# Output projections of a two-layer decoder trunk with the weights stationary and the residual stream as features by tokens

## The chip, the core and the metric

The kernel runs on one core of a Trainium2 chip. The core has five engines with queues of their own: TensorE (PE, with its weight loads shown apart as PEld) multiplies 128x128 stationary blocks with moving blocks of up to 512 columns into PSUM; VectorE (DVE), ScalarE (ACT) and GpSimd (POOL) work on tiles of 128 partitions; SyncE (SP) issues most DMA transfers. SBUF holds the tiles, PSUM has eight banks of 128 x 512 float32, DRAM holds inputs, outputs and a few intermediate tensors. The metric is the device time of one execution in microseconds, as the median of several runs.

## What is computed

A trunk of two layers over x (512 tokens x 2048 features, float32). Layer 0 mixes tokens by retention with 8 heads, layer 1 by latent attention (MLA) with 16 heads. Each layer is a normalised and modulated sub-layer with a gated residual add:

```python
c_act = jax.nn.silu(c)
for i in range(DEPTH):
    mod = (c_act @ ada_w[i] + ada_b[i])[:, None, :]
    shift, scale, gate = jnp.split(mod, 3, axis=-1)
    h = rmsnorm(x, norm_g[i]) * (1.0 + scale) + shift
    j = i // N_MIXERS
    if i % N_MIXERS == 0:
        y = retention_branch(h, positions, ret_w_in[j], ret_gn_g[j], ret_w_out[j])
    else:
        y = mla_branch(h, positions, mla_w_in[j], mla_q_norm_g[j], mla_w_uq[j],
                       mla_kv_norm_g[j], mla_w_ukv[j], mla_w_out[j])
    x = x + gate * y
return rmsnorm(x, final_norm_g)
```

Each branch ends in an output projection: `(silu(g) * y) @ w_out`, 4096 x 2048 in layer 0 and 2048 x 2048 in layer 1.

## The kernel before

**Precision.** Every operand is held as a high and a low part (hi, lo) in a reduced float32 form; `split` makes them with a ScalarE copy (hi, L132) and a VectorE subtraction (lo, L133). A product is three PE passes: hi x hi, hi x lo, lo x hi.

**The sequence.** Layer 0's input projections come first, with 7 products where 8 would be needed for value and gate. Then a list of `Step` objects is worked off (loop at L1499). A step has units of weights (a load on SP's queue and a `prepare`, which splits), a `multiply` for PE, a `follow` for what comes after it, and work placed `beside` it. In step i the loop loads up to three units ahead, prepares the units of step i + 1, does the `form` work on VectorE and ScalarE, multiplies, and then follows. `behind` and `queued` place instructions behind the last one on the named engines; what is written without them the framework may order by its own estimate of readiness.

**Modulation.** `ada_w` is 2048 rows by 6144 columns per layer. `later_modulation` (L840) takes it in pieces of 1024 columns: 16 loads of 512 KB (one row per partition) on SP's queue, and for each one VectorE operation that adds it, scaled by c_act, to `am` (L857). `Step.rows` says how many such loads a step asks for; their additions come in the next step. Buffers for the rows are `bw`, two of them. `sum_modulation` (L863) then sums `am` over the partitions on PE: for shift and scale by eight matmuls of one column (L870), for the gate by two broad products with a block of ones (L877), whose first row goes with the bias through DRAM (`gate_d`) and comes back spread over all partitions. The last two pieces (layer 1's gate) are loaded during the last two gate blocks of layer 2's input (`g23`, L1460, 16 steps), with one row in the first four steps and two in each of the other twelve; what is left is loaded behind the loop (L1546), and the sum stands there too (L1549), ahead of the attention of the first pair of heads in the text (`uq_chunk`, `ukv_chunk`).

**First output projection (o1).** Four rounds n over pairs of heads, each with four column groups r of 512 features (`round_steps`, L1143). The activations `o1_in` (features by tokens) are the stationary operand, in blocks of 128 tokens; the weights move, 512 features wide (`o1_product`, L1133). So a bank holds 128 tokens x 512 features. In the last round groups 3 and 2 end in `x1_out` (L1110): multiply by the gate, add the residual x, square with a sum per token, write x1 to DRAM. Groups 0 and 1 are done together with weights 1024 wide (`wide`): four steps for the first four units, then four steps with one block of tokens each (`one_token`), so that token blocks finish one after the other.

**Between the layers.** `x1_scale` normalises each block of tokens in place, `h2_pair` (L1238) transposes it on PE (four 128x128 transposes per feature block and half of the tokens) and forms the hi and lo parts of h2, modulated, for 256 tokens at a time. The gate projection of layer 2 (`ga`) starts on half of the tokens: `ga_half` multiplies a unit of weights with 256 columns. `front` (L1380) interleaves these halves with the transposes and with `kr_half` (rotary key).

**Second output projection (o2).** `out_projection` (L1553) does the same as o1 with one round: column groups 0 and 1 alone, 2 and 3 together with the last four units (`tail=4`) done bank by bank. `evac` multiplies by the gate and adds x1; `x2_out` squares, sums per token and multiplies by the final gain; `x2_token` (L1811) takes a block of 128 tokens when all its groups are there, computes the factor (POOL's power at L128), scales 2048 features on ScalarE and VectorE and writes them out.

PSUM banks come in two sets of four, `acc` and `aux`.

## Time and profile before

| | us |
|---|---|
| median of 3 runs | 2253.04 (2251.67 to 2254.42) |
| the profiled execution, as a run | 2254.86 |
| its span, first to last instruction | 2253.1 |
| mean granted TensorE clock | 0.989 of full |

The profile is of one execution. A page gives busy times by engine, the span in 40 slices, and the chain of work that ended last; other views list who waited for whom, busy time in chosen windows, groups of equal instructions with their mean time, and single instructions in order of time. In such rows a line number (L1139) is that of the kernel before; `o<-o_whi,o_h` is output and inputs by their names without numbers; a square bracket at the end gives the idle time ahead of an instruction and what ended it. PE's instructions overlap: a matmul is shown with 0.39 us though the next starts 0.23 us after it.

### The profile page before, as it was taken

Reading aid. Unit: us, or ns where it says so; the run is one execution under the profiler, and the core shown is the slowest. Engines: PE = TensorE matmul, PEld = TensorE weight load, DVE = VectorE, ACT = ScalarE, POOL = GpSimd, SP = SyncE. Lnnn points to the kernel's source line nnn. Section 1 sums busy time; section 2 is a strip of 40 time slices with the busy share of each in tenths; the row PEclk is TensorE's granted clock in tenths of the full one; section 3 lists DMA queues with packets and bytes.
Section 4 is the critical chain, followed back from the end, with each engine's and each line's share of the span. In section 5 each row is a group of like instructions: output and inputs, shape, how many; then the busy total and the mean of one; then the engine's idle time right before and its main releaser. Section 6 shows DMA issues by size and latency. Waiting matters only on the chain.

```text
span 2253.1 us, 28084 instructions
## 1 busy us (share of the span) xinstructions
PE 2178.4 (97%) x10238; PEld 1812.8 (80%) x10238; DVE 1601.9 (71%) x2389; ACT 1012.1 (45%) x1526; POOL 113.9 (5%) x201
## 2 busy tenths in 40 slices
PE   5999999999999999999999999989999799999997
PEld 4887888888888888888888888868888588888886
DVE  7988867766676789666777776656867667777545
ACT  5664433434343454434344444454454155555433
POOL 1000000100000000000000000010001000000000
PEclk9999999999999999999999999989999899999999
DMA  9974685767767778664555555633556822235433
GB/s 342 347 241 159 191 296 188 265 217 242 242 218 255 241 247 288 196 203 153 201 185 189 177 182 174 209 100 99 170 194 218 278 80 80 85 98 173 150 126 117
DMA packets 237340, 440.29 MB, mean 195 GB/s; under 512 B 21561, under 2 KB 95377, under 8 KB 237201
## 3 DMA queue, kind: packets, MB, share of 16 engines
q1 hardware_dynamic: 224192, 399.31, 54.6%
q0 software_dynamic: 12576, 38.91, 4.3%
q8 instruction: 80, 1.31, 0.2%
q14 instruction: 60, 0.48, 0.1%
q10 hardware_dynamic: 432, 0.27, 0.0%
HBM read 395.41 MB, written 43.01 MB: 195 GB/s over the span
## 4 chain that ended last, share of the span: by engine, by line
PE 72%; DVE 12%; DMA 7%; ACT 5%; issue 4%; POOL 0%; SPq 0%; ACTq 0%; DVEq 0%; POOLq 0%
PE o L1139 12%; PE qk L160 4%; PE qk L158 4%; PE qk L159 4%; DMA aw<-in_ada_w_dram 2%; DMA mod_aw<-in_ada_w_dram 2%; PE o L158 2%; PE o L160 2%; PE o L159 2%; PE x L696 2%; PE y L696 2%; PE x L697 2%; PE y L697 2%; PE y L695 2%; PE x L695 2%
## 5 line engine op out<-in xcount | busy, mean ns | idle before, releaser
L1139 PE MATMUL o<-o_whi,o_h 128*128 128x512 f32 x488 | 191.0, 391 | 0.0
L1139 PE MATMUL o<-o_whi,o_l 128*128 128x512 f32 x488 | 189.9, 389 | 0.0
L1139 PE MATMUL o<-o_wlo,o_h 128*128 128x512 f32 x488 | 189.9, 389 | 0.0
L857 DVE SCALAR_TENSOR_TENSOR mod_am<-mod_aw,cact,mod_am 128x1024 f32<-128x1024 f32 x120 | 153.6, 1280 | 34.9 <-DMA mod_aw<-in_ada_w_dram 34.8
L158 PE MATMUL qk<-hT,qk_h 128*128 128x512 f32 x448 | 175.3, 391 | 0.0
L160 PE MATMUL qk<-hT,qk_l 128*128 128x512 f32 x448 | 174.6, 390 | 0.0
L159 PE MATMUL qk<-hT,qk_h 128*128 128x512 f32 x448 | 174.3, 389 | 0.0
L133 DVE TENSOR_TENSOR o_wlo<-o_r,o_whi 128x1024 fp32r<-128x1024 f32 x61 | 74.6, 1223 | 75.3 <-ACT o_whi L132 75.3
L133 DVE TENSOR_TENSOR qk_l<-qk_r,qk_h 128x1024 fp32r<-128x1024 f32 x56 | 68.0, 1222 | 64.0 <-ACT qk_h L132 63.7
L1139 PEld LDWEIGHTS o<-o_whi,o_l 128*128 128x128 f32 x488 | 91.6, 188 | 19.2
L1139 PEld LDWEIGHTS o<-o_wlo,o_h 128*128 128x128 f32 x488 | 91.7, 188 | 18.5
L1139 PEld LDWEIGHTS o<-o_whi,o_h 128*128 128x128 f32 x488 | 91.7, 188 | 18.5
L158 PE MATMUL o<-o_w_hi,o_h 128*128 128x512 f32 x256 | 100.1, 391 | 0.0
L159 PE MATMUL o<-o_w_lo,o_h 128*128 128x512 f32 x256 | 99.8, 390 | 0.0
L160 PE MATMUL o<-o_w_hi,o_l 128*128 128x512 f32 x256 | 99.5, 390 | 0.0
L160 PEld LDWEIGHTS qk<-hT,qk_l 128*128 128x128 f32 x448 | 84.1, 188 | 18.5 <-DVE qk_l L133 1.1
L159 PEld LDWEIGHTS qk<-hT,qk_h 128*128 128x128 f32 x448 | 84.1, 188 | 17.8 <-issue 0.5
L158 PEld LDWEIGHTS qk<-hT,qk_h 128*128 128x128 f32 x448 | 84.1, 188 | 17.7 <-ACT qk_h L132 0.2
L132 ACT CAST qk_h<-qk_r 128x1024 fp32r<-128x1024 f32 x56 | 57.9, 1049 | 88.5 <-PE qk L159 73.4
L370 DVE SCALAR_TENSOR_TENSOR am<-aw,cact,am 128x512 f32<-128x512 f32 x118 | 88.7, 752 | 3.6
L160 PE MATMUL g<-h,g_l 128*128 128x512 f32 x232 | 90.6, 391 | 0.6 <-DVE g_l L133 0.6
L158 PE MATMUL g<-h,g_h 128*128 128x512 f32 x232 | 91.0, 392 | 0.0
(1266 smaller groups left out, 5890.8 us busy)
## 6 DMA issues: line engine op xcount, KB each, us to landing
mod_aw<-in_ada_w_dram SPq DMA_DIRECT2D x128, 512.0 KB, 5.3
aw<-in_ada_w_dram SPq DMA_DIRECT2D x128, 256.0 KB, 6.0
o_r<-in_ret_w_out_dram SPq DMA_DIRECT2D x64, 512.0 KB, 4.4
qk_r<-in_ret_w_in_dram SPq DMA_DIRECT2D x112, 256.0 KB, 3.9
g_r<-in_mla_w_in_dram SPq DMA_DIRECT2D x32, 512.0 KB, 4.4
o_w_raw<-in_mla_w_out_dram SPq DMA_DIRECT2D x32, 512.0 KB, 3.7
qk_d<-qk_st POOLq DMA_DIRECT2D x32, 256.0 KB, 4.0
qk_r<-qk_d SPq DMA_DIRECT2D x32, 256.0 KB, 6.1
```

The costliest lines, as they stand in the source:

```text
L132: ACT.copy(hi, src)
L133: DVE.tensor_sub(lo, src, hi.bitcast(F32))
L158: PE.matmul(o, lhs[0], rhs[0], start=first and not seeded, stop=False, skip_group_check=seeded)
L159: PE.matmul(o, lhs[0], rhs[1], start=False, stop=False, skip_group_check=seeded)
L160: return PE.matmul(o, lhs[1], rhs[0], start=False, stop=last, skip_group_check=seeded)
L370: DVE.scalar_tensor_tensor(out=am, in0=aw[:, k % 2], scalar=ck, in1=am, op0=ALU.mult, op1=ALU.add)
L695: PE.matmul(banks[b], a[0], w[0], start=first, stop=False, skip_group_check=True)
L696: PE.matmul(banks[b], a[0], w[1], start=False, stop=False, skip_group_check=True)
L697: PE.matmul(banks[b], a[1], w[0], start=False, stop=True, skip_group_check=True)
L857: DVE.scalar_tensor_tensor(out=am, in0=aw, scalar=ck, in1=am, op0=ALU.mult, op1=ALU.add)
L1139: PE.matmul(o, a[i], w[j][:, ki, cols], start=first and i + j == 0, stop=last and i == 1, skip_group_check=True)
```

## The change

The residual stream is kept as features by tokens in both output projections, so that 128 features stand on the partitions of a bank and 512 tokens along it:

- Weights are the stationary operand, activations the moving one. x is also handed over transposed (`x_t`), and the output comes in blocks (half of the tokens, 256 features) that the host only rearranges.
- The gate of a layer is a column of 128 features per block (`gate_c`), summed like shift and scale; its way through DRAM and the loads that spread it go. Gate and residual add are one fused VectorE operation (`scalar_tensor_tensor`).
- The sum of squares per token is a sum over partitions: squares are added up in one tile (`ss1`, `ss2`), `token_sums` sums it with matmuls of one column, `token_factors` forms the inverse roots and puts them on diagonals, `spread` multiplies ones with a diagonal, which leaves the factor of each token on all partitions of a bank.
- h2 needs no transposes: `h2_pair` takes two feature blocks for half of the tokens, by fused operations with the factor from PSUM.
- The last columns (four units of weights) are done by halves of the tokens, 256 columns each: `tail0` to `tail3` in o1, `o2_end` in o2, with the norm of the first half among the products of the second.
- `front` has three steps; kr is loaded, multiplied (all tokens at once) and used later.
- The rows of the last two pieces of `ada_w` are asked for two to a step from the first of the 16 steps, with buffers `bw` and `pt` in turn (`pt` has four); the last sum stands behind `uq_chunk` and `ukv_chunk` of the first pair.
- `form_input` and `latent_parts` form the low part by one fused operation.

```diff
-    def later_modulation(pool, pieces, tags=("bm", "bw")):
+    def later_modulation(pool, pieces, tags=("bm", (("bw", 2),))):
...
+            ps = aux(f"{name}_ps")
+            for b in range(8):
+                PE.matmul(ps[:, b : b + 1], am[:, b // 4, b % 4 * P : (b % 4 + 1) * P], crow, start=True, stop=True)
...
+    def token_sums(ps, ss, n0, n):
+        for t in range(n0, n0 + n):
+            PE.matmul(ps[:, t : t + 1], ss[:, t * P : (t + 1) * P], crow, start=True, stop=True)
+
+    def token_factors(ps, n0, n, name):
+        r = rsqrt(ps[:, n0 : n0 + n], n, 1.0 / D, name)
+        diag = tmp(f"{name}_diag")
+        for t in range(n):
+            DVE.tensor_scalar(
+                out=diag[:, t * P : (t + 1) * P], in0=ident, scalar1=r[:, t : t + 1], scalar2=None, op0=ALU.mult
+            )
+        return diag
+
+    def spread(ps, diag, n0, n):
+        for t in range(n):
+            PE.matmul(ps[:, (n0 + t) * P : (n0 + t + 1) * P], ones, diag[:, t * P : (t + 1) * P], start=True, stop=True)
...
-    def x1_out(r, t):
-        g, v = tmp(f"o1_g{r}_{t}"), x1_block(t, r)
-        DVE.tensor_mul(g, o1_banks[3, r, t], o1_gates[r])
-        DVE.tensor_add(v, g, o1_res[t, r])
-        junk = tmp(f"x1_sq{t}_{r}")
-        ACT.activation(junk, v, AF.Square, accum_out=ss1[t][:, r : r + 1])
-        POOL.dma_start(x1_d[t * P : (t + 1) * P, r * T : (r + 1) * T], v)
+    def x1_out(r, b, half=None):
...
+        DVE.scalar_tensor_tensor(
+            out=v, in0=o1_banks[3, r, b][:, cols], scalar=gate_c[0][:, kt : kt + 1], in1=o1_res[b, r][:, cols],
+            op0=ALU.mult, op1=ALU.add,
+        )
+        if half != 0:
+            POOL.dma_start(x1_d[kt * P : (kt + 1) * P, :], whole_)
...
+        sq = tmp(f"x1_sq{r}_{b}_{half}")[:, cols]
+        ACT.activation(sq, v, AF.Square)
+        return lambda: DVE.tensor_add(ss1[0][:, cols], ss1[0][:, cols], sq)
...
-                o, a[i], w[j][:, ki, cols], start=first and i + j == 0, stop=last and i == 1, skip_group_check=True
+                o, w[i][:, ki, c0 + b * P : c0 + (b + 1) * P], a[j], start=first and i + j == 0, stop=last and i == 1,
...
+    block[3].follow = lambda: outs(3, range(4))
+    def second_out():
+        outs(2, range(4))
+        for b in range(4):
+            seed(3, 1, b)
+    block[7].follow = second_out
...
+    def norm_sums(half):
+        if half == 0:
+            norm2["s"] = aux("x1_sums")
+        token_sums(norm2["s"], ss1[0], 2 * half, 2)
...
+    def h2_pair(u, half):
...
+            DVE.scalar_tensor_tensor(
+                out=t, in0=x1[u][:, kt % 2, cols], scalar=a_col[1][:, kt : kt + 1], in1=norm2["r"][:, cols],
+                op0=ALU.mult, op1=ALU.mult,
+            )
...
+            ACT.activation(hi, t, AF.Identity, bias=b_col[1][:, kt : kt + 1])
...
+                DVE.scalar_tensor_tensor(
+                    out=lo, in0=t, scalar=b_col[1][:, kt : kt + 1], in1=hi.bitcast(F32), op0=ALU.add, op1=ALU.subtract
+                )
...
+    def tail2():
+        tail_block(1, 0, 1)
+        queued(out_behind, 1, 0, 1)
+        norm_sums(0)
+        queued(norm_factors, 0)
+        tail_block(1, 1, 1)
+        queued(out_behind, 1, 1, 1)
+        tail_block(1, 2, 1)
+        norm_spread(0)
+        queued(out_behind, 1, 2, 1)
+        lows = queued(h2_pair, 0, 0)
+        tail_block(1, 3, 1)
+        queued(out_behind, 1, 3, 1)
+        queued(lows)
...
+    def front0():
+        ga_half(0, 0)
+        norm_sums(1)
+        queued(norm_factors, 1)
+        queued(h2_pairs, (2, 0))
+        ga_half(1, 0)
+        norm_spread(1)
+        queued(h2_pairs, (0, 1), (1, 1), (2, 1))
+
+    front = [Step() for _ in range(3)]
...
+    front[1].multiply = lambda: (ga_half(2, 0), ga_half(0, 1), queued(h2_pairs, (3, 0), (3, 1), (4, 0)))
+    front[2].multiply = lambda: (ga_half(1, 1), ga_half(2, 1), queued(h2_pairs, (4, 1), (5, 0), (5, 1)))
+    steps += front + ga[3:]
+    ga[3].beside["form"].append(lambda: h2_pairs((6, 0), (6, 1)))
+    ga[4].beside["form"].append(lambda: h2_pairs((7, 0), (7, 1)))
+    ga[6].units.append((kr_load, kr_prepare))
+    ga[6].beside["multiply"].append(kr_products)
...
-    g23 = g2_steps(2, rows=lambda u: 1 if u < 4 else 2) + g2_steps(3, rows=lambda u: 2)
+    g23 = g2_steps(2, rows=lambda u: 2) + g2_steps(3, rows=lambda u: 2)
...
-        yield from later_modulation(pools["l2"], [(1, 2, n) for n in range(2)])
+        yield from later_modulation(pools["l2"], [(1, 2, n) for n in range(2)], ("bm", (("bw", 2), ("pt", 4))))
...
-    sum_modulation(0)
-    use_modulation()
...
     run(uq_chunk(0, *tiles_[:2]))
     run(ukv_chunk(0, *tiles_[2:]))
-    pending = None
+    sum_modulation(0)
+    use_modulation()
...
+    def o2_out(kt, ps, half=None):
...
+        DVE.scalar_tensor_tensor(
+            out=v, in0=ps[:, cols], scalar=gate_c[1][:, kt : kt + 1], in1=o2_res[kt][:, cols],
+            op0=ALU.mult, op1=ALU.add,
+        )
...
+            sq = tmp(f"x2_sq{kt}_{half}")[:, cols]
+            ACT.activation(sq, v, AF.Square)
+            DVE.tensor_add(ss2[:, cols], ss2[:, cols], sq)
+        ACT.activation(v, v, AF.Identity, scale=final_c[:, kt : kt + 1])
...
+    def o2_final(half):
+        cols = slice(half * H, (half + 1) * H)
+        for j in range(KD // 2):
+            v = x2[j][:, :, cols]
+            DVE.tensor_mul(v, v, factor2[:, cols].unsqueeze(1).to_broadcast([P, 2, H]))
+            nc.sync.dma_start(out[half, j], v)
+
+    for b in range(8):
+        o2_end(b, 0)
+    o2_end(0, 1)
+    sums2_ = acc("x2_sums")
+    token_sums(sums2_, ss2, 0, 2)
+    diag = token_factors(sums2_, 0, 2, "x2_0")
+    o2_end(1, 1)
+    factor2 = acc("x2_r")
+    o2_end(2, 1)
+    spread(factor2, diag, 0, 2)
+    o2_final(0)
+    for b in range(3, 8):
+        o2_end(b, 1)
+    token_sums(sums2_, ss2, 2, 2)
+    spread(factor2, token_factors(sums2_, 2, 2, "x2_1"), 2, 2)
+    o2_final(1)
```

`tail0` and `tail1` do the first half of the tokens for groups 1 and 0, `tail3` the second half for group 0 with `h2_pair(1, 0)` between its blocks; each `tail_block` is four units by three passes, 256 columns wide. `o2_end` is the same for a bank of o2 and calls `o2_out`.

457 lines of the change are left out of this document (210 added, 247 removed).

## The prediction

> **What bounds the kernel now.** I read the page first: the busy shares, the granted clock and the chain.
>
> ```profile
> PE 2178.4 (97%) x10238; PEld 1812.8 (80%) x10238; DVE 1601.9 (71%) x2389; ACT 1012.1 (45%) x1526; POOL 113.9 (5%) x201
> PEclk9999999999999999999999999989999899999999
> PE 72%; DVE 12%; DMA 7%; ACT 5%; issue 4%; POOL 0%; SPq 0%; ACTq 0%; DVEq 0%; POOLq 0%
> ```
>
> TensorE (PE) is busy for 97% of the span, so time can only come from fewer matmul columns or from the few places where PE stands still. 2253.1 - 2178.4 = 74.7 us are idle in all. Two of the forty slices have a lower clock; the second view, PE's waits, says why.
>
> ```profile
> PE xT_ps L476 <- ACT x L453: 17.5, 4, 10.5
> PE mod_ps L877 <- DVE mod_am L857: 10.7, 1, 10.7
> PE x1T L1246 <- DVE h2f L1263: 8.9, 3, 5.7
> PE pT L1689 <- ACT p L1676: 5.5, 7, 0.9
> ```
>
> The first belongs to the start and the fourth to attention, which the diff leaves alone. The second (the sum of the modulation) and the third (the transposes of the residual stream between the layers) stand at lines that it rewrites. The third view gives both places, a dense stretch for comparison, and the end.
>
> ```profile
> 1480.00:1510.00 30.00, 19.85 (x91) 15.52 (x90) 18.97 (x37) 15.36 (x30) 5.65 (x10) 0.80 0.33 114
> 1730.00:1750.00 20.00, 20.00 (x88) 16.26 (x88) 12.98 (x12) 5.96 (x9) 2.70 (x5) 1.00 0.90 315
> 1790.00:1810.00 20.00, 10.83 (x31) 7.35 (x32) 10.84 (x11) 3.70 (x7) 1.00 (x2) 0.62 0.52 168
> 2240.00:2253.10 13.10, 0.00 (x0) 0.00 (x0) 5.72 (x13) 3.63 (x6) 1.54 (x2) 0.59 0.40 160
> ```
>
> Columns: length, busy time of PE, weight load, DVE, ACT and POOL, clock, DMA share, GB/s. PE is idle for 10.2 us in the first window, 9.2 us in the third and all 13.1 us at the end; after an idle stretch its clock is low too (0.80, 0.62).
>
> **The swap of operands itself is free.** Weights become the stationary operand and activations the moving one; both remain 128x128 against 128x512, three passes each. Units and splits stay as they are, so rounds 0 to 2 of the first output projection and most of the second cost what they cost. Edits with no price, since PE's products cover them: form_input and latent_parts lose one operation of about 0.7 us per block, o2_out has two VectorE operations where three stood (a block's last products take 1.36 us), the gate's trip through DRAM and its eight broadcast loads go, kr's load and products move three steps later and are needed only there. Without that cover o2_out would cost 0.7 us for each block less, never more. These rows give the prices, from one start to the next:
>
> ```profile
> 2237.46 0.39 PE L160 MATMUL o<-o_w_hi,o_l 128*128 128x512 f32 x1
> 2238.14 0.39 PE L160 MATMUL o<-o_w_hi,o_l 128*128 128x512 f32 x1
> 1513.34 0.40 PE L1334 MATMUL g<-h,g_h 128*128 128x256 f32 x2
> 1513.70 0.40 PE L1334 MATMUL g<-h,g_h 128*128 128x256 f32 x2
> ```
>
> Three passes of 512 columns take 0.68 us (0.227 each), three of 256 columns 0.36 us (0.12 each). "Last columns by halves" turns 96 passes into 192 in each projection: 192 x 0.12 - 96 x 0.227 = **+1.3 us, twice**.
> The Trainium skill, "TensorE: Matmul & The Clock Gate", section "Back-to-back issue gap", would make it less: N / 2.4 + 2.5 ns, 109 ns for 256 columns and 216 ns for 512, hence +0.3 us twice and a sum 2 us lower. The rows stand closer to this kernel's fp32 halves, so I keep them.
>
> **Between the layers.** Here PE ends layer 1 and starts the gate projection of layer 2:
>
> ```profile
> 1494.33 0.39 PE L1139 MATMUL o<-o_whi,o_l 128*128 128x512 f32 x1
> 1494.56 0.60 PE L1246 MATMUL x1T<-ident,x 128*128 128x128 f32 x4
> 1510.53 0.78 PE L1334 MATMUL g<-h,g_h 128*128 128x256 f32 x2
> 1540.68 1.03 PE L1246 MATMUL x1T<-ident,x 128*128 128x128 f32 x8
> 1541.47 0.48 PE L158 MATMUL g<-h,g_h 128*128 128x512 f32 x1
> ```
>
> From 1494.56 to 1510.53 PE only transposes or waits: 16.0 us. The other 40 transposes go in five groups of eight, each 0.79 us or a little more (1540.68 to 1541.47): 4.3 us; the cold restart costs about 0.5 us. Removed: **20.8 us**.
>
> What comes instead: the square sums are added over partitions by tiny matmuls, the factor is spread by two 128-column matmuls for each half, and VectorE scales. By the halves' price the 16 added passes are 2 us, with 1.3 us for the 256-column blocks. kr's 64 passes of 256 become 32 of 512: -0.4 us. The new waits I found by walking the queues with these rows:
>
> ```profile
> L1264 DVE TENSOR_TENSOR h<-h2f,h 128x256 fp32r<-128x256 f32 x32 | 12.8, 423 | 13.9 <-ACT h2f L1261 13.4
> L1263 DVE TENSOR_SCALAR h2f<-x1T,a_col,b_col 128x256 f32<-128x256 f32 x16 | 8.7, 543 | 0.3
> L1259 ACT ACTIVATE h<-x1T,b_col,a_col 128x256 fp32r<-128x256 f32 x32 | 17.3, 580 | 12.3 <-PE x1T L1246 12.3
> L133 DVE TENSOR_TENSOR g_l<-g_r,g_h 128x1024 fp32r<-128x1024 f32 x32 | 38.9, 1222 | 15.8 <-ACT g_h L132 15.7
> L1025 DVE SCALAR_TENSOR_TENSOR y<-yT,vcol,sg x4: 745/746/753, 1035.7 to 1039.5; 128x512 f32<-128x512 f32 x4
> 2240.82 0.99 POOL L128 TENSOR_TENSOR x_r<-x_v,mhalf 128x1 f32<-128x1 f32 x1 [5.47 <-DVE x_v L126]
> ```
>
> A half block is 12 passes, 1.44 us on PE. On DVE its x1_out costs a fused operation and an add, 2 x 0.42 = 0.84 us, and each h2 pair four fused operations. No row has the fused operation at 256 columns; it lies between 0.42 (the plain one at 256) and 0.75 us (the fused one at 512, PSUM operand included). I take 0.46, since it reads as many columns as the first row. In tail2 norm_sums(0) takes an aux bank that x1_out(1, 0, 1) must first read; on DVE that stands behind the last x1_out of half 0 and a weight split of 1.22 us, so PE waits about 1.7 us, and behind it all of tail2 does. norm_sums(1) waits 0.3 us after ga_half(0, 0), ga_half(2, 0) 0.6 us for pair (2, 0). Then DVE is ahead: from the start of tail2, pairs 0 to 5 come to 48 x 0.46 + 6.7 (eight x1_out) + 3.2 (two factors, POOL's power in each) + 7.3 (six splits) = 39.3 us, and PE needs pair 5 after eight half blocks, six half units, two whole units and the small products, 11.5 + 17.3 + 10.9 + 2 = 42 us. Waits: 3 us (0 to 13). Added 1.3 + 2 - 0.4 + 3 = 5.9 us: **net -14.9 us**.
> The Trainium skill, "PSUM — Partial Sum Buffer", section "PSUM bank collisions raise a hardware error", says that two engines must not touch one bank in the same partitions at once. norm_spread(1) writes the bank from which DVE reads half 0 for pair (2, 0); kept apart by that rule, PE would wait for the pair's first two operations, and the sum would be 1 us higher. No run so far shows such a pair.
>
> ACT stays below DVE (eight squares and 24 copies of at most 0.58 us, by its row above); the removed in-place scaling waited for x1's DMA, and nothing takes that place. seed(3, 1) now stands behind four squares on ACT instead of one each, and so do the next weights' casts: +0.3 us. The transposed x costs the same 16 loads; three more small loads on POOL and 48 more columns of one copy lie before the start's first weights: nothing.
>
> **The gate of layer 2.**
>
> ```profile
> 1785.17 0.39 PE L159 MATMUL uq<-qT,uq_hi 128*128 128x512 f32 x1
> 1797.74 1.28 DVE L857 SCALAR_TENSOR_TENSOR mod_am<-mod_aw,cact,mod_am 128x1024 f32<-128x1024 f32 x1 [1.68 <-DMA mod_aw<-in_ada_w_dram]
> 1799.17 3.75 PE L877 MATMUL mod_ps<-mod_am,ones 128*128 128x512 f32 x4 [10.70 <-DVE mod_am L857]
> 1801.94 1.42 PE L158 MATMUL uq<-qT,uq_hi 128*128 128x512 f32 x1
> 1807.44 0.40 PE L158 MATMUL uk<-kvT,ukv_hi 128*128 128x512 f32 x1
> mod_aw<-in_ada_w_dram SPq DMA_DIRECT2D x128, 512.0 KB, 5.3
> 925.19 1.84 PE L870 MATMUL mod_ps<-ones,mod_am 128*128 128x1 f32 x16
> 926.89 0.49 PE L695 MATMUL x<-vg_13o_h,hT 128*128 128x512 f32 x1
> ```
>
> From 1785.40 (one pass after the first row) to 1807.44 PE does 16 passes of uq, worth 3.6 us, in 22.0 us: 18.4 us lost. The reason is in the rows' plan: 4 + 8 + 16 = 28 of 32 rows of ada_w are asked for in the 16 steps, the last four follow afterwards, each waiting for its DMA, and the sum (and uq behind it) for the last. The change asks for two from the first step, 32 of 32, with bw and pt buffers in turn, and places the sum behind uq and ukv of pair 0, some 19 us of PE work. The sum as columns takes 1.70 us and a slow start behind it, 1.95 us. DMA: two rows and one unit are 3 x 512 KB in 24 passes, 5.44 us: 289 GB/s, with the gate's writes some 313; the window 1730 to 1750 carries 315 with PE fully busy, so four more such steps should hold. I leave 1 us for a late split: **net -15.5 us** (-7 to -16). The other three gate pieces cost 0.2 us more each as columns than as two broad products: +0.6 us.
>
> **The end.**
>
> ```profile
> 2239.50 0.39 PE L160 MATMUL o<-o_w_hi,o_l 128*128 128x512 f32 x1
> 2247.39 1.15 ACT L1815 ACTIVATE x<-x,x_r 128x1024 f32<-128x1024 f32 x1 [1.64 <-POOL x_r L128]
> L1809 DVE TENSOR_TENSOR x<-x,fg 128x512 f32<-128x512 f32 x16 | 11.0, 689 | 6.7 <-ACT x_sq L1808 6.7
> ```
>
> Today 13.2 us follow the last product. Afterwards: half 0 is scaled by eight multiplies of 0.69 us, 5.5 us on DVE, while PE does five half blocks, 7.2 us. Behind them DVE has five o2_out, 4.4 us if the next fused operation fills the wait for ACT, 6.6 us if not; then sums, POOL's power (0.99), diagonal, spread, 3.3 us; eight multiplies again, 5.5 us; last write 3.4 to 4.5 us (from 2248.54 to the end it is 4.6 us today for twice the bytes). That is 15.7 to 18.8 us behind the last product: +4. PE gets 1.3 us of halves and 1.4 us of sums, spread and a bank wait. **Net +6.7 us** (+4 to +12).
>
> **Sum**, against the profiled execution: -14.9 + 0.3 - 15.5 + 0.6 + 6.7 = -22.8 us of 2253.1 us. That execution took 2254.86 us as a run, 1.8 us above the median of 2253.04; I subtract from the median: **2230 us**.
>
> **Rivals.**
> *The gate's wait only shrinks (2239 us).* The window 1750 to 1770, whose DMA has slack on paper, ran at 265 GB/s:
>
> ```profile
> 1750.00:1770.00 20.00, 20.00 (x85) 15.71 (x85) 12.62 (x12) 4.12 (x4) 1.45 (x3) 1.00 0.77 265
> ```
>
> At that rate a step's loads need 5.9 us against 5.44, 8 us over 16 steps, and PE gets its weights that much later. Against it: PE was full in that very window. The sum not being moved, since instructions seem not to run in the order of the text (uq went ahead of the sum), would cost no more, because the four late rows are gone. 0.12.
> *VectorE takes over between the layers (2242 us).* If the fused operation costs 0.75 us at 256 columns too, pairs 0 to 5 take 53 us, 11 us behind PE, and the last two add 2 x (8 x 0.75 + 1.22 - 5.44) = 3.5 us; 2.5 us of that are waits already counted. For it: L1263 is 28% dearer than L1264 at equal columns. Against: the plain operation falls from 0.69 us (L1809, at 512) to 0.42 (L1264). 0.12.
> *The same place, slower than before (2266 us).* VectorE becomes the bound outright, at 1.1 us per fused operation when one operand stands in PSUM and PE writes beside it: pairs 0 to 5 need 70 us against 42, the last two 9 us more, 36 us of new waiting. From about 0.95 us on it makes the kernel slower by over 0.2%. No row shows such a price (0.75 at 512 with PSUM). 0.08.
>
> **The numbers.** Forecast 0.68, with 2222 to 2238 us as its own range; rivals 0.12, 0.12, 0.08. 0.2% is 4.5 us, about what a measurement of this kernel tells from no change. The upper end, 2245, takes in the first two rivals; with all new waits gone and the end at its cheaper bound it is 2223, and 2220 leaves 3 us below that for VectorE's lighter queue, which I can't price. Faster by over 0.2%: the forecast and nearly all of the first two rivals, 0.86. Slower: 0.08. The rest, where the end and a rival add up, 0.06.
>
> **What would show it.** Right: no PE wait over 2 us between the last o1 product and ga[3]; mod_ps behind ukv of pair 0 without a wait; windows around both at a clock of 1.00; 15 to 19 us behind the last product. Wrong: PE waiting for h2 in ga[3] to ga[7] (VectorE), for g_l or uq_lo before attention (DMA), or a fused operation at 256 columns over 0.6 us.

## The result, and the profile after

The changed kernel takes **2223.68 us** in the median of 4 runs (2223.08 to 2225.20), the kernel before 2252.73 beside it; the ratio is 0.9871 (95% interval 0.9854 to 0.9888), 29.05 us less. The forecast was 2230, with a range from 2220 to 2245. The profiled executions span 2221.8 and 2253.1 us, 31.3 us apart: the one of before lies 2.1 us above the median of its runs, the one of after at its median. The forecast's sum, -22.8 us, was made against the profiled execution of before; measured the same way, between the two profiles, 8.5 us more were saved than that.

The page of the changed kernel (busy times; the clock in 40 slices; the chain of waits by engine):

```profile
PE 2170.8 (98%) x10414; PEld 1819.9 (82%) x10414; DVE 1586.6 (71%) x2397; ACT 998.5 (45%) x1496; POOL 104.2 (5%) x184
PEclk9999999999999999999999999999999999999998
PE 75%; DVE 11%; ACT 5%; issue 5%; DMA 2%; POOL 0%; SPq 0%; DVEq 0%; POOLq 0%; ACTq 0%
```

PE is busy for 7.6 us less, although it has 176 instructions more on record; most of the saving, 23.7 of the 31.3 us, is idle time (74.7 us before, 51.0 after). The two slices with a low clock are gone; the 8 in the last slice is the end, where PE has nothing left to do. Of PE's waits (total, times, longest) the two at mod_ps (10.7) and x1T (8.9) that stood second and third are gone too, and these are what the change brings:

```profile
PE xT_ps L482 <- ACT x L459: 17.2, 4, 10.9
...
PE x_sums L891 <- DVE x_ss L1841: 2.6, 1, 2.6
PE x_r L906 <- DVE x_diag L898: 1.4, 1, 1.4
PE x_r L906 <- DVE h2f L1276: 1.2, 1, 1.2
...
PE x_sums L891 <- DVE x L1127: 0.2, 1, 0.2
```

The first is the old one of the start. To see where the time went, I cut both executions at the same products of PE's timeline. After:

```profile
1058.62 0.39 PE L1161 MATMUL o<-o_h,o_whi 128*128 128x512 f32 x1
...
1493.75 0.28 PE L1161 MATMUL o<-o_h,o_wlo 128*128 128x256 f32 x1
1493.87 0.40 PE L1426 MATMUL g<-h,g_h 128*128 128x256 f32 x2
1593.11 0.50 PE L701 MATMUL xc<-vgc_00e_h,h 128*128 128x512 f32 x1
1761.46 0.39 PE L158 MATMUL uq<-qT,uq_hi 128*128 128x512 f32 x1
2007.42 0.39 PE L160 MATMUL uk<-kvT,ukv_lo 128*128 128x512 f32 x1
2205.78 0.28 PE L1861 MATMUL o<-o_h,o_w_lo 128*128 128x256 f32 x1
```

And before (the last product there is at 2239.50, shown above):

```profile
1059.91 0.39 PE L1139 MATMUL o<-o_whi,o_h 128*128 128x512 f32 x1
1611.65 0.50 PE L695 MATMUL xc<-vgc_00e_h,h 128*128 128x512 f32 x1
1780.86 0.39 PE L158 MATMUL uq<-qT,uq_hi 128*128 128x512 f32 x1
2043.49 0.39 PE L160 MATMUL uk<-kvT,ukv_lo 128*128 128x512 f32 x1
```

The cuts are the first product of the first output projection, the first of layer 2's c projection, the last uk of pair 7, the last product of the second output projection, and the end of the span. S1 holds the first output projection and the place between the layers, S2 the gate of layer 2, S3 and S4 the end. Differences of these starts, in us:

| stretch | before | after | difference | forecast |
|---|---|---|---|---|
| S0, to the first o1 product | 1059.91 | 1058.62 | -1.3 | +0.4 |
| S1, to the first c product | 551.74 | 534.49 | -17.3 | -14.6 |
| S2, to the last uk | 431.84 | 414.31 | -17.5 | -15.3 |
| S3, to the last o2 product | 196.01 | 198.36 | +2.4 | +2.7 |
| S4, to the end | 13.60 | 16.02 | +2.4 | +4.0 |
| sum | 2253.10 | 2221.80 | -31.3 | -22.8 |

(The forecast column sorts the prediction's terms: S0 two gate pieces of 0.2; S1 -14.9 and +0.3; S2 -15.5 and one piece; S3 the end's PE work; S4 what follows it.) Three windows of the changed kernel at those places (length, busy time of PE, weight load, DVE, ACT, POOL, then clock, DMA share, GB/s):

```profile
1490.00:1520.00 30.00, 28.80 (x215) 27.45 (x214) 27.83 (x65) 15.74 (x33) 3.29 (x6) 1.00 0.37 124
1790.00:1810.00 20.00, 19.35 (x110) 16.08 (x109) 17.27 (x45) 13.85 (x31) 0.54 (x1) 1.00 0.16 54
2212.00:2221.80 9.80, 0.09 (x1) 0.00 (x0) 4.87 (x8) 0.00 (x0) 0.00 (x0) 0.50 0.62 214
```

PE stands still for 1.2 us of the first where it was idle for 10 before, and the clock is 1.00 where it was 0.80 and 0.62. In the first window DVE is busy for 27.8 of 30 us: that is the new neighbour of the limit.

### The profile page after: what moved, and what is told of

It is laid out like the page before. It is cut to its first block, busy times and chain, and to the rows that moved or that the text cites. A ratio compares the mean times of both kernels' runs of the same rounds, so it can differ in the third digit from the quotient of the medians.

```text
span 2221.8 us, 28357 instructions
## 1 busy us (share of the span) xinstructions
PE 2170.8 (98%) x10414; PEld 1819.9 (82%) x10414; DVE 1586.6 (71%) x2397; ACT 998.5 (45%) x1496; POOL 104.2 (5%) x184
## 4 chain that ended last, share of the span: by engine, by line
PE 75%; DVE 11%; ACT 5%; issue 5%; DMA 2%; POOL 0%; SPq 0%; DVEq 0%; POOLq 0%; ACTq 0%
PE o L1161 13%; PE qk L160 4%; PE qk L158 4%; PE qk L159 4%; PE o L1861 4%; DVE am L376 2%; PE x L702 2%; PE y L703 2%; PE x L703 2%; PE y L701 2%; PE y L702 2%; PE x L701 2%; PE s L703 2%; PE s L702 2%; PE s L701 2%
## 5 line engine op out<-in xcount | busy, mean ns | idle before, releaser
L1161 PE MATMUL o<-o_h,o_whi 128*128 128x512 f32 (+1 forms) x496 | 192.5, 388 | 0.0
L1161 PE MATMUL o<-o_h,o_wlo 128*128 128x512 f32 (+1 forms) x496 | 191.6, 386 | 0.0
L1161 PE MATMUL o<-o_l,o_whi 128*128 128x512 f32 (+1 forms) x496 | 191.5, 386 | 0.0
L1161 PEld LDWEIGHTS o<-o_h,o_wlo 128*128 128x128 f32 x496 | 93.2, 188 | 18.7
L1161 PEld LDWEIGHTS o<-o_l,o_whi 128*128 128x128 f32 x496 | 93.3, 188 | 18.3
L1161 PEld LDWEIGHTS o<-o_h,o_whi 128*128 128x128 f32 x496 | 93.3, 188 | 18.1
L159 PEld LDWEIGHTS qk<-hT,qk_h 128*128 128x128 f32 x448 | 84.1, 188 | 17.3
L158 PE MATMUL g<-h,g_h 128*128 128x512 f32 x232 | 90.7, 391 | 0.3 <-ACT g_h L132 0.3
L159 PE MATMUL g<-h,g_h 128*128 128x512 f32 x232 | 90.4, 389 | 0.0
L132 ACT CAST o_whi<-o_r 128x1024 fp32r<-128x1024 f32 x61 | 63.5, 1052 | 21.9 <-issue 10.1
L133 DVE TENSOR_TENSOR o_w_lo<-o_w_raw,o_w_hi 128x1024 fp32r<-128x1024 f32 x32 | 38.9, 1220 | 34.6 <-ACT o_w_hi L132 34.5
```

The source lines that it names most:

```text
L132: ACT.copy(hi, src)
L133: DVE.tensor_sub(lo, src, hi.bitcast(F32))
L158: PE.matmul(o, lhs[0], rhs[0], start=first and not seeded, stop=False, skip_group_check=seeded)
L159: PE.matmul(o, lhs[0], rhs[1], start=False, stop=False, skip_group_check=seeded)
L1161: PE.matmul(o, w[i][:, ki, c0 + b * P : c0 + (b + 1) * P], a[j], start=first and i + j == 0, stop=last and i == 1, skip_group_check=True,)
```

## Experiments

E1 to E12 are twelve kernels: E1 is built from the kernel before, the others from the changed one. S1 to S4 of their profiled executions, and the medians of their runs:

| run | S1 | S2 | S3 | S4 | median us |
|---|---|---|---|---|---|
| E1 gate alone, on before | 551.89 | 415.91 | 196.02 | 13.61 | 2239.38 |
| E2 row count undone | 536.16 | 414.18 | 198.38 | 15.89 | 2223.85 |
| E3 buffers undone | 534.49 | 415.41 | 198.38 | 16.30 | 2226.40 |
| E4 place undone | 534.55 | 414.18 | 198.38 | 15.98 | 2224.38 |
| E5 place alone | 536.18 | 422.56 | 198.33 | 16.31 | 2233.33 |
| E6 count alone | 536.19 | 424.51 | 198.36 | 16.22 | 2234.08 |
| E7 buffers alone | 536.19 | 414.41 | 198.39 | 16.29 | 2224.37 |
| E8 form_input, all on VectorE | 539.56 | 414.24 | 198.39 | 16.30 | 2229.67 (one) |
| E9 first projection whole | 543.18 | 414.10 | 198.32 | 15.89 | 2232.14 |
| E10 second projection whole | 536.19 | 414.07 | 195.88 | 24.30 | 2231.26 |
| E11 h2 twice, form_input as before | 550.54 | 414.20 | 198.33 | 15.84 | 2240.48 |
| E12 own bank, late finals | 535.78 | 414.14 | 198.33 | 17.10 | 2226.17 |

Where a stretch holds the same code it repeats within 0.3 us in S2 (414.07 to 414.31) and 0.1 us in S3, so half an us can be read from one profile where a run's time would hide it. S1 has a second value, 1.7 us up; the last section tells where it comes from.

**The gate of layer 2 (E1 to E7).** Three edits went into it: two rows of ada_w from the first step, six buffers instead of two, and the sum behind uq and ukv of pair 0. The short diffs against the changed kernel:

```diff
 E2, E5, E7 (row count undone)
-    g23 = g2_steps(2, rows=lambda u: 2) + ...
+    g23 = g2_steps(2, rows=lambda u: 1 if u < 4 else 2) + ...
 E3, E5, E6 (buffers undone)
-    ("bm", (("bw", 2), ("pt", 4)))
+    ("bm", (("bw", 2),))
 E4, E6, E7 (place undone)
+    sum_modulation(0); use_modulation()
     run(uq_chunk(0, *tiles_[:2])); run(ukv_chunk(0, *tiles_[2:]))
-    sum_modulation(0); use_modulation()
```

E1 puts all three into the kernel before.

> The kernel before with the gate part alone: two rows of ada_w from the first of the sixteen steps, six buffers in turn instead of two, the sum behind uq and ukv of pair 0; the gate stays a broadcast row that goes through DRAM. Theory: this part carries 16 us by itself, as in the traces (uk of pair 0 starts 18.5 us earlier relative to uq, less 2 us for the sum): 2236 to 2238 us, PE without a wait over 1 us at uq and mod_ps. Rival: the 16 us come only together with the columns instead of the broadcast row, then 2242 us or more. Up to 1750 us this kernel runs what the kernel before runs, so its profile also tells whether the profiled execution of before, 2.1 us above the median of its runs, was long in one place: the first product of the first output projection starts at 1059.9 us in that profile and at 1058.6 in the one after; theory, that 1.3 us is chance: 1058.6 +- 0.5 here; rival, the change shortens the start: 1059.9 +- 0.5.

> The changed kernel with the row count of before: one row in each of the first four steps, so 28 of 32 rows are asked for in the steps and four behind them; buffers and place of the sum as changed. The prediction's step (the last four rows are what was late): about 10 us or more of PE's waiting come back, 2234 us or more. Rival (the six buffers let the queue run ahead; the last row of the changed kernel is added at 1753 us, 8 us ahead of uq): the four rows come 6 us later, nothing waits for them, 2223 to 2226 us.

> The changed kernel with two buffers for the rows of ada_w in layer 2 instead of six; row count and place of the sum as changed. Rival to the prediction's step (the buffers do it): with two buffers a row's load waits until the row two before it is added, SP's queue falls behind, and the weights of uq and ukv stand behind the rows on that queue: PE waits 10 to 20 us in sum between the end of the gate products and the second pair, 2233 to 2244 us. The prediction's step (the row count does it): 2223 to 2226 us.

> The changed kernel with the sum of the last gate piece ahead of uq of pair 0, where it stood before; row count and buffers as changed. Theory: in the changed kernel the last row is added at 1753 us and uq starts at 1761.5, so the sum finds its rows: 2223 to 2226 us, no wait over 1 us at mod_ps. Rival (the place hides the wait): 8 us or more come back, 2231 us or more.

E1: ratio 0.9939 (0.9924 to 0.9954), 13 us, a little less than expected; in the trace S2 falls by 15.9 us, nearly all of the 17.5. The 1.6 us that it misses lie ahead of uq: from the first c product to the first product of uq it takes 170.0 us (before 169.2, changed kernel 168.35), and PE waits 1.7 us there for an evacuation on ACT (L1311) that had itself waited for a DMA. Behind uq, E1 and the changed kernel take the same, 245.9 and 246.0 us (before 262.6), so the gate as a row shows no cost there. Its start, 1060.77, fits neither expectation; see S0 below. E2, E3 and E4 had ratios of 0.9871 (0.9857 to 0.9886), 0.9886 (0.9869 to 0.9902) and 0.9874 (0.9859 to 0.9888): undoing any one of the three gives back 1.1 us of S2 (E3) or nothing. E2's rival and E4's theory hold, E3's 10 to 20 us do not come (two of its four runs, without a trace, took 2228 and 2229 us; why is open). So none of them is needed, and the question becomes which is enough.

> The changed kernel with two buffers and with the row count of before, so that of the three edits to the gate only the place of the sum is left. E1 to E4 show that no single one of the three is needed; this run and the next two ask which one is enough. Theory (the place alone is not enough): the rows come as late as before, 18 us behind the start of uq, and the splits of uq's and ukv's second units stand behind their additions on VectorE; PE waits for these splits instead of for the sum, 8 to 10 us: 2231 to 2235 us. Rival (the sum behind 19 us of PE work hides all): 2223 to 2226 us.

> Two buffers and the sum ahead of uq as before; only the row count is changed (32 of 32 in the steps). In E3 the last row was added at 1766 us, 5 us behind the start of uq. The prediction's step (the four late rows were the reason): 2223 to 2225 us. Theory (the count takes some 13 us of the lateness, not all): PE waits 2 to 5 us at mod_ps or uq_lo, 2226 to 2229 us.

> Row count of before (four rows follow behind the steps) and the sum ahead of uq as before; only the six buffers are left. Theory (two buffers were the reason: a row's load waited for the addition two rows before it, so the queue ran behind): in E2 the last row was added at 1757 us with this plan, 4 us ahead of uq; no wait over 1 us at mod_ps, 2223 to 2226 us. The prediction's step (the late rows were the reason): 10 us of waiting come back, 2232 us or more.

The ratios are 0.9901 (0.9884 to 0.9918), 0.9911 (0.9896 to 0.9926) and 0.9870 (0.9855 to 0.9884). Of the 17.5 us the place alone brings 9.3, the count alone 7.3, and the **buffers alone 17.4**: E5 and E7 as the theory said, E6 with 5 us more than it allowed. Each of the three figures holds what the other edits of the change bring to S2 (0.9 us ahead of uq), since no run of the changed kernel undoes all three; in E1, where the three stand without the others, they bring 15.9. PE's wait in E5, then in E6:

```profile
PE uk L160 <- DVE ukv_lo L133: 3.7, 2, 1.9
```

```profile
PE mod_ps L876 <- DVE mod_am L864: 6.6, 1, 6.6
```

With the place alone the sum no longer holds up PE, but the splits of ukv stand on VectorE behind the late rows' additions; with the count alone PE stands at the sum as before, for less. The rest of each loss is the slower clock around the wait: 0.83 from 1770 to 1800 us in E5, 0.74 from 1760 to 1780 us in E6, some 5 us each, of which a part fell into the waits themselves. How the additions run tells the cause: 30 of them (shortest, median, longest ns; first and last start), before, and what VectorE waited for ahead of them; then the same line in E7:

```profile
L857 DVE SCALAR_TENSOR_TENSOR mod_am<-mod_aw,cact,mod_am x30: 1264/1284/1286, 1696.0 to 1797.7; 128x1024 f32<-128x1024 f32 x30
...
  DMA mod_aw<-in_ada_w_dram: 26.9, 21
```

```profile
L864 DVE SCALAR_TENSOR_TENSOR mod_am<-mod_aw,cact,mod_am x30: 1273/1284/1287, 1678.2 to 1757.8; 128x1024 f32<-128x1024 f32 x30
```

The same 28 rows of 32 are planned into the steps in both. With two buffers a row's load must wait until the row two before it is added, and VectorE waits in turn for that load, 21 times; the chain needs 101.7 us from its first start to its last and ends 18 us behind the start of uq (1797.7 and the last 1.3 us, against 1780.9). With six it needs 79.6 us, VectorE waits for no row, and it ends 4.6 us ahead of uq's start (1763.7, against 1757.8 and the last 1.3 us). The four late rows are no hindrance then. An estimate from these rows fits: a load takes 5.3 us to land (median) and an addition 1.3 us, and with two buffers two rows share such a round trip of 6.6 us, 3.3 us for each; 101.7 us for 29 steps from row to row are 3.5. With six it is 2.7 us a row.

**form_input (E8, and the second half of E11).**

```diff
-    DVE.scalar_tensor_tensor(out=lj, in0=ps, scalar=gn, in1=hj, op0=mult, op1=subtract)
+    f = tmp(...)
+    DVE.tensor_scalar(out=f, in0=ps, scalar1=gn, op0=mult)     # E11: ACT.activation for odd j
+    DVE.tensor_sub(lj, f, hj)
```

> The changed kernel with form_input's VectorE work as before: a scaled copy and a subtraction instead of the one fused operation per block. The prediction gave this edit no price. In the traces the stretch from the first product of the first output projection to the last head's transposes takes 347.1 us before and 345.7 after, in two jumps of 0.7 us where PE waited for VectorE's low part of v. Theory: the extra operation is what is late; the two waits of 0.4 us for v are back and the stretch takes 347.1 us. Rival: other queue order or chance; 345.7 us.

E8 did more than its expectation says: before, ScalarE made every second scaled copy, so E8 puts 2.7 us more on VectorE for a head, where the kernel before had 1.4. The stretch, at a clock of 1.00, takes 350.7 us (1059.41 to 1410.13), 5.0 more than in the changed kernel and more than either side expected (E11's expectation says 5.9; 0.8 of that lies ahead of the stretch). PE's waits for v, in E8, before, and after:

```profile
PE y L159 <- DVE v L133: 3.7, 4, 1.3
```

```profile
PE y L159 <- DVE v L133: 0.8, 2, 0.4
```

```profile
PE y L159 <- DVE v L133: 0.3, 2, 0.2
```

E11 made the exact undoing: 347.1 us (1058.49 to 1405.61), as before (347.13), against 345.68 in the changed kernel. So the one operation less is worth 1.4 us there, and 2.7 us of VectorE work for a head cost 3.6 times as much as 1.4 us of it (5.0 us).

**VectorE between the layers (E11).**

```diff
     DVE.scalar_tensor_tensor(out=t, in0=x1, scalar=a_col, in1=r, op0=mult, op1=mult)
+    DVE.scalar_tensor_tensor(out=t, in0=x1, scalar=a_col, in1=r, op0=mult, op1=mult)
```

> Two edits in stretches that the trace keeps apart. (1) The fused operation of h2 runs twice, 32 x 0.40 us = 12.6 us more on VectorE between the layers. The prediction's reading (VectorE stays ahead of PE): the stretch from the last product of the first output projection to the first product of the c projection grows by 4 us at most (99.4 us in the changed kernel). Rival (VectorE is at its limit there): by 9 us or more. (2) form_input has the operations of the kernel before: two VectorE operations and one ScalarE operation more per head. E8, which put in twice the VectorE work, lost 5.9 us between 1058 and 1410 us. Theory (VectorE's work in form_input is on the path): the stretch from the first product of the first output projection to the last transposes, 345.7 us in the changed kernel, takes 347 to 347.3 us, as before. Rival: 346 us or less.

From the last o1 product to the first c product it takes 114.2 us (1494.80 to 1609.03) against 99.4: **+14.9 us** for 12.6 us of doubled work; the ratio is 0.9950 (0.9933 to 0.9966). The expectation of 4 us at most falls, the rival holds. Some 10 us of it are PE's waits in that stretch (1.5 in the changed kernel), most of them for casts of the gate's weights on ACT (6.1) and for the second spread (2.6); much of the rest is the clock, 0.66 and 0.86 in two of the windows below. Three windows of the changed kernel, then of E11:

```profile
1505.00:1515.00 10.00, 10.00 (x80) 9.74 (x80) 10.00 (x25) 5.98 (x13) 0.00 (x0) 1.00 0.07 13
1515.00:1525.00 10.00, 10.00 (x46) 8.29 (x45) 10.00 (x23) 5.99 (x13) 0.00 (x0) 1.00 0.40 99
1525.00:1535.00 10.00, 10.00 (x46) 8.29 (x45) 9.52 (x17) 5.45 (x9) 0.00 (x0) 1.00 0.48 154
```

```profile
1505.00:1515.00 10.00, 9.45 (x56) 9.45 (x57) 9.25 (x23) 3.70 (x8) 0.00 (x0) 0.66 0.09 33
1515.00:1525.00 10.00, 7.43 (x54) 6.59 (x53) 9.30 (x21) 4.28 (x8) 0.00 (x0) 1.00 0.03 5
1525.00:1535.00 10.00, 7.32 (x27) 5.62 (x26) 9.26 (x22) 4.33 (x9) 0.00 (x0) 0.86 0.21 64
```

In the changed kernel PE and DVE are both busy for 10.00 of 10.00 us in the first two windows. PE does not wait there, but VectorE has next to nothing left; my expectation had counted the pairs alone and left out that the gate's weights are split on the same queue. ACT, busy for 4 of 10 us in E11, is not the limit: it waits 27.9 us for the fused operations of h2 between 1494 and 1550 us, and its casts stand behind those waits.

**Whole columns instead of halves (E9, E10).** E9 computes the last units of the first projection on 512 columns, with the whole norm behind them; E10 does the same in the second.

```diff
 E9
-    o1_product(..., slice(half * H, (half + 1) * H), u == 7)
+    o1_product(..., slice(0, T), u == 7)
 ... (tail2, tail3 and front0: the norm and the first pairs behind the products)
 E10
-    for b in range(8): o2_end(b, 0)
-    ... (o2_end(b, 1) with sums, spread and o2_final(0) among them)
+    for b in range(8): o2_end(b, None)
+    token_sums(sums2_, ss2, 0, 4); spread(factor2, token_factors(sums2_, 0, 4, ...), 0, 4)
+    o2_final(0); o2_final(1)
```

> The changed kernel with whole columns of 512 tokens in the last units of the first output projection, the norm behind them, and the gate projection of layer 2 behind the norm. Theory (the halves hide the norm's chain): 96 passes fewer starts save 1.3 us, and PE stands from the last product until the first h2 pair: last fused operation, square and add 2.1 us, sums to spread 3.5 us, first pair 2.5 us, about 8 us, nothing more behind it: 2229 to 2232 us. Rival (VectorE's queue is what counts, so whole columns with fewer, longer operations cost nothing): 2222 to 2225 us.

> The changed kernel with whole columns of 512 tokens in the last units of the second output projection and one norm behind them. In the changed kernel 2 MB of output are written at 340 GB/s in the last 8 us. Theory (the write sets the end): first final multiply 6 us behind the last product, then 4 MB at 340 GB/s, 12.3 us, and 3.5 us around it: 22 us behind the last product against 16; PE ends 2 us earlier; 2227 to 2229 us. Rival (VectorE's multiplies set the end, 16 x 0.61 = 9.8 us): 19 us behind the last product, 2224 to 2226 us.

E9: 0.9909 (0.9894 to 0.9924), as the theory said, 8.5 us above the changed kernel. From its last product (and that product's 0.2 us) to the gate's first one PE has only the sums and the spread, 9.2 us:

```profile
1490.91 0.39 PE L1161 MATMUL o<-o_h,o_wlo 128*128 128x512 f32 x1
1493.87 1.05 PE L891 MATMUL x_sums<-ones,x_ss 128*128 128x1 f32 x8 [2.57 <-DVE x_ss L1139]
...
1500.36 1.61 PE L1409 MATMUL g<-h,g_h 128*128 128x256 f32 x5 [1.12 <-ACT h L1283]
```

E10: 0.9906 (0.9891 to 0.9921). PE ends 2.5 us earlier, and the end comes 24.3 us behind it, not 22: the first final multiply came 8.4 us behind the start of the last product (2207.70 to 2216.07) instead of 6 (6.35 in the changed kernel). The sums and the spread take four blocks of tokens there instead of two, 1.86 and 2.07 us against 0.81 and 1.22, both at about half the clock (0.52 from 2210 to 2215 us in E10, 0.54 from 2208.6 to 2212.2 us in the changed kernel). From there the write sets the end, as the theory said: 15.9 us, against 9.6 us of multiplies.

```profile
2220.00:2225.00 5.00, 0.00 (x0) 0.00 (x0) 5.00 (x9) 0.00 (x0) 0.00 (x0) 0.50 1.00 344
2225.00:2230.00 5.00, 0.00 (x0) 0.00 (x0) 0.72 (x2) 0.00 (x0) 0.00 (x0) 0.50 1.00 344
```

DVE is nearly done in the second window (0.72 us) while the DMA engines still run at 344 GB/s. So the halves are worth 7 us in the first projection (its 8.7 us of S1, less the 1.7 us of the clock told in the last section; the clock behind PE's pause, 0.74 from 1490 to 1510 us, is in it) and 5.8 us in the second (S3 and S4).

**A version from these readings (E12).**

```diff
-    if half == 0: norm2["r"] = aux("x1_r")
-    spread(norm2["r"], norm2["diag"], 2 * half, 2)
+    norm2["r", half] = aux(f"x1_r{half}")
+    spread(norm2["r", half], norm2["diag"], 2 * half, 2)
 ...
-    o2_final(0)
-    for b in range(3, 8): o2_end(b, 1)
+    for b in range(3, 8): queued(o2_final, 0, b - 3, b - 2); o2_end(b, 1)
     token_sums(sums2_, ss2, 2, 2)
-    spread(factor2, token_factors(sums2_, 2, 2, "x2_1"), 2, 2)
+    diag = token_factors(sums2_, 2, 2, "x2_1")
+    queued(o2_final, 0, 5, 8)
+    spread(factor2, diag, 2, 2)
```

> A version made from the readings: the second half's factor is spread into a PSUM bank of its own, and of the first half's eight final multiplies one stands ahead of each of the last five o2_out and three behind the last, where VectorE waits for the norm. Theory: the wait of 1.2 us at the second spread goes; the last square sum is added 1.2 us earlier, so the sums start 1.5 us behind the last product instead of 2.8 and the end comes 1.2 us earlier; 2.4 us in all: 2220.5 to 2222 us. Rival (the three multiplies behind the last o2_out delay the diagonal, or their writes the last writes): the end stays within 0.4 us, 2222.5 to 2223.5 us.

It is not better: 0.9883 (0.9869 to 0.9898), no difference from the changed kernel that these runs can tell, and outside the ranges of both expectations. The wait of 1.2 us at the second spread between the layers is gone (0.3 and 0.4 us are left beside it; S1 gains 0.4 us on the kernels with the same clock). At the end the sums did start 0.7 us earlier (2.2 us behind the start of the last product, 2.9 before), but the spread then waited, and S4 grew by 1.1 us. VectorE and PE of E12:

```profile
2209.43 0.48 DVE L898 TENSOR_SCALAR x_diag<-ident,x_r 128x128 f32<-128x128 f32 x2 [0.87 <-POOL x_r L128]
2209.83 1.87 DVE L1882 TENSOR_TENSOR x<-x,x_r 128x512 f32<-128x512 f32 x3
```

```profile
2211.76 1.22 PE L906 MATMUL x_r<-x_diag,ones 128*128 128x128 f32 x4 [3.40 <-DVE x L1882]
```

The diagonal is there at 2209.9; the spread starts at 2211.76, when the three moved multiplies (to 2211.70) have read the first half's factor: it is in the bank that the spread writes. I gave the layers' factor a bank of its own and left the end's in one. With a second bank there the spread could start some 1.9 us earlier, and the multiplies behind it 1.3 us at most, since VectorE is busy until 2211.70; that version was not run.

## Why the prediction was right, and where its sizes were off

Faster, inside the range, and on its main mechanism: PE stood still at two places and no longer does, with no wait over 1.2 us between the layers and none at the last mod_ps, as the prediction's signs asked. Its reason for the second place was wrong all the same. Point by point:

- **The swap of operands is free, and the edits with no price.** Right for the products: with form_input as before, rounds 0 to 2 of the first projection take 347.12 us in E11 and 347.13 before. The step that failed is "Edits with no price, since PE's products cover them", which names form_input and latent_parts: form_input measures -1.4 us (E11), since VectorE's queue delivers v to the next head. The S2 share ahead of uq (-0.9 us, where a wait of 0.6 us for the gate's split is gone) may be the same through latent_parts; that is only argued, no run undoes it alone.
- **The halves' price.** Right: the rows 1493.75 and 1493.87 are 0.12 us apart, and S3 grew by 2.4 us for a forecast of 2.7. The formula of the Trainium skill, "TensorE: Matmul & The Clock Gate", section "Back-to-back issue gap", which that page gives for an isolated matmul, comes out 11 ns too low for these passes at both widths (109 against 120, 216 against 227); by it the halves would cost an estimated 0.2 us each time, where the prediction wrote 0.3.
- **Between the layers.** Removed as forecast: the gate's first product follows 0.12 us behind the last one, where 16 us stood. Of the added "Waits: 3 us" 1.4 came. The failed step is "behind it all of tail2 does":

```profile
1480.63 0.28 PE L1161 MATMUL o<-o_h,o_big 128*128 128x256 f32 x1
1484.76 0.61 PE L891 MATMUL x_sums<-ones,x_ss 128*128 128x1 f32 x4 [0.25 <-DVE x L1127]
```

  tail2's first half block starts at 1480.63, and 31 passes (3.88 us), not 12 (1.44 us), run ahead of the sums: PE's order is not the text's, 7 of the 12 passes of the third half block went first. So 1.7 us became 0.25. The other two waits, 0.3 and 0.6, did not come. What did come is the one that the prediction put beside its sum: the second spread starts at 1501.43, when VectorE has read half 0 for pair (2, 0), 1.2 us late (1 us forecast). It goes when that half has its own bank (E12), and E12's end shows the same wait at another place. Both fit the rule of the Trainium skill, "PSUM — Partial Sum Buffer", section "PSUM bank collisions raise a hardware error", that the software must keep two engines' accesses to one bank apart. A bank is one tile of the program here, so the runs don't tell whether the wait is made for the bank or for the tile. Together with form_input these are -1.4, -1.5, -0.9 and +1.2, about the 2.7 us by which S1 beat its forecast.
- **VectorE's share.** "Then DVE is ahead" was right by little. The fused operation at 256 columns lasts 0.475 us (0.46 taken), but in a row they start 0.39 us apart (four in the 1.57 us between these two starts):

```profile
L1276 DVE SCALAR_TENSOR_TENSOR h2f<-x,a_col,x_r 128x256 f32<-128x256 f32 x32 | 13.5, 475 | 0.0
```

```profile
1512.98 1.65 DVE L1276 SCALAR_TENSOR_TENSOR h2f<-x,a_col,x_r 128x256 f32<-128x256 f32 x4
1514.55 0.88 DVE L1288 SCALAR_TENSOR_TENSOR h<-h2f,b_col,h 128x256 fp32r<-128x256 f32 x2
```

  E11 shows what the lead was: 12.6 us more cost 14.9. The rival "VectorE takes over" did not happen, but it was the right one to fear, and its price looks low: at 0.75 us instead of 0.475 the 64 fused operations of h2 would add 17.6 us of work, more than E11 did.
- **The gate of layer 2.** Size nearly right (S2 -17.5 for -15.3; 16.7 of it behind uq, where 15.3 were forecast and the late split of 1 us did not come), reason wrong. The failed step is "The reason is in the rows' plan: 4 + 8 + 16 = 28 of 32". The reason was the two buffers: E7 keeps that plan and gains all. The size came out because it was read from the time that PE lost, whatever the reason, and because the buffers happened to be among the edits; that part is luck. The rival of a shrinking wait at 265 GB/s falls with it: the queue ran far ahead and the last row was added at 1753.1 us, 8 us ahead of uq.
- **The end.** +4.8 us for +6.7. The 15.7 to 18.8 us behind the last product came out at 16.0; I had charged the middle. VectorE did fill ACT's gaps (2208.59 less 2204.43, 4.2 us for what I put at 4.4 to 6.6), and the write took over from the multiplies: in these windows

```profile
2214.00:2216.00 2.00, 0.00 (x0) 0.00 (x0) 2.00 (x5) 0.00 (x0) 0.00 (x0) 0.50 0.98 332
2216.00:2218.00 2.00, 0.00 (x0) 0.00 (x0) 1.00 (x2) 0.00 (x0) 0.00 (x0) 0.50 1.01 343
2218.00:2220.00 2.00, 0.00 (x0) 0.00 (x0) 0.00 (x0) 0.00 (x0) 0.00 (x0) 0.50 0.99 346
```

  the DMA engines are full until 2220, 3 us behind the last multiply.
- **S0** was forecast at +0.4 and came at -1.3. The twelve kernels after it, eleven of them with the changed kernel's own start, reach the same product between 1057.2 and 1061.6 us; this is chance, and no part of the change. In these two profiles most of it is one draw of the clock: from 175 to 185 us it is 0.83 before and 1.00 after, worth 1.7 us, and the two profiles, 0.3 us apart at 170 us, are 1.4 us apart at 203 us.

So the sum erred to one side: charges for waits that did not come (1.5, 0.9, 1.0), an edit taken at nothing (1.4) and the end (1.9) make 6.7 us, the wait of 1.2 us takes some back, and the 1.7 us between S0 and its forecast and the 0.9 us ahead of uq are most of the rest of the 8.5 us. Subtracting from the median, 2.1 us below that profile, took some off the other way, by luck: the result lies 6.3 us under the forecast.

## What to carry to other kernels

When a wait ends on a chain of load and add, count the buffers before the loads: a chain that holds two at a time moves two in each round trip, and here four buffers more did by themselves what a new plan and a new place were added for. An edit that takes one operation from an engine which feeds PE is not free where PE waits for that engine, and the busy share does not tell where: in form_input's stretch VectorE was busy for only 71% (241 of the 340 us from 1060 to 1400), and an edit still moved PE by 1.4 us. Read PE's waits, and the busy share in windows of 10 us, not over the span. And a half that is written into a bank which another engine still reads for the other half is no half.

## What the hardware showed unasked

At a sum of the modulation at 1406 us PE idles for 0.25 us between 16 transposes and 16 passes of one column. In the window around it the granted clock was 0.91 in some executions and 1.00 in others, of the same code and with PE busy alike; the first line is the changed kernel's, the second that of E2:

```profile
1400.00:1420.00 20.00, 19.75 (x104) 16.71 (x103) 9.54 (x16) 4.73 (x7) 0.00 (x0) 1.00 0.31 105
```

```profile
1400.00:1420.00 20.00, 19.75 (x96) 16.49 (x96) 8.36 (x15) 4.43 (x7) 0.00 (x0) 0.91 0.31 99
```

It costs 1.7 us (3.41 us at half the clock), the second value of S1 (E2, E5, E6, E7, E9, E10 and E12 have it). The wait of 0.25 us is there in all fourteen traces, so it is not the whole cause. The traces' records of the clock show more: every stretch between two changes in the middle of a trace is a whole multiple of 3.41 us, so the changes stand on a raster of that step. Counted on it, carried back from the drop at the kernel's end, the wait ends 0.5 to 1.6 us behind a step in the seven executions that have the drop, and 1.8 to 3.2 us, once 0.0, in the seven that don't. The position on the raster thus separates the two groups; why it does is not shown. So a small shift of everything ahead can decide such a price, and a difference of one or two us between two profiles has to be looked up in the clock before it is given to an edit.
